# Bonus sums behind the preparation, a new column order of the key tile, and small copies on GpSimd, in a hybrid RWKV-7 and RG-LRU block

## The chip, the core and the metric

The kernel runs on one core of a Trainium2 chip. The metric is device microseconds of one execution, lower is better. Five engines take part, each with its own queue of instructions: TensorE (PE, matrix products; PEld is its loading of weights), VectorE (DVE), ScalarE (ACT), GpSimd (POOL) and SyncE (SP, which only issues transfers here). DMA transfers move data between the chip's memory (HBM) and the core's on-chip memory (SBUF); products land in PSUM, of which the kernel uses eight banks of 128 partitions by 512 floats. Instructions on an engine run in their queue's order; semaphores order the engines among each other.

## What is computed

The block maps x (512 frames by 1024 channels, float32) through a mixer with two branches, a cross-attention to 256 memory rows and a gated convolutional feed-forward layer. The change lies in the first branch, RWKV-7, with 8 heads of 64 channels:

```python
p = p + (token_shift(p) - p) * mu
r, k, v = p[..., :c0], p[..., c0:c1], p[..., c1:c2]
...
w_log = -jax.nn.softplus(-(w0 + jnp.tanh(pw) @ w_up)) - 0.5
decay = jnp.exp(-jnp.exp(w_log))
a = jax.nn.sigmoid(a0 + pa @ a_up)
...
kk = k * k_k
k = k * (1.0 + (a - 1.0) * k_a)
...
kk = kk / jnp.maximum(jnp.sqrt(jnp.sum(kk * kk, axis=-1, keepdims=True)), 1e-12)
y = rwkv7_recurrence(r, decay, k, v, -kk, kk * a)
...
y = ((y - mean) * lax.rsqrt(var + LNX_EPS)).reshape(bsz, s, A_WIDTH) * lnx_g + lnx_b
bonus = jnp.sum(r * k * r_k, axis=-1, keepdims=True) * v
return (y + bonus.reshape(bsz, s, A_WIDTH)) * g
```

The recurrence is S_t = S_{t-1} diag(w_t) + (S_{t-1} a_t) b_t^T + v_t k_t^T with y_t = S_t r_t, where −kk stands for a and kk·a for b. The keys k and the "betas" b = kk·a of the title are the last two factors of the recurrence; the bonus is a sum over a head's 64 channels, times v. The second branch is a causal convolution with a gated linear recurrence (RG-LRU). Both are merged by gates, and the rest of the block follows.

## The kernel before

**Layout.** Activations lie channels by frames. Four pairs of heads (j = 0 to 3) fill 128 partitions each, one head (e = 0 or 1) in each half. The 512 frames are cut into 8 chunks of 64.

**Projections.** `inproj(i)` computes 128 output columns of `h @ w_in` into one PSUM tile `in_ps{i}`: 24 matmuls, since each float32 product is made of three with rounded parts (high times high, high times low, low times high; lines 160 to 162). A weight tile arrives by DMA (`win_r`), is rounded on ACT (`win_h`, L114), and DVE subtracts for the low part (`win_l`, L115); three buffers hold the high parts and three the low ones. Tiles `in_ps` share three PSUM banks. `evac_shift` (L521 to L525) evacuates one: it fills column 0 of `q` (L523), ACT writes the shifted rest of `q` (L524), and DVE combines `q` with the PSUM tile (L525) into `pk` (k), `pr` (r) or `vT` (v). `q` has two buffers, which `sq` uses too. The columns are taken in the order 12, 13, 4, 5, 0, 1, 8, 9 (k, r, v of pairs 0 and 1), 6, 7, 2, 3, 10, 11 (pairs 2 and 3), then the other branches' from 22 on.

**Preparation of a pair.** `prep(j)` makes the low-rank products `psw` and `psa` (L547, L548, four matmuls), the cumulated log decay by a scan (L553), its exponentials `Pp` and `L` and the decay of each chunk, `PC` (L558). `prep2(j)` normalises kk (the sum `ss`, L156 and L157), and fills `AK` (the left factors: −kk and r with decay) and `KBt` (betas and keys with the inverse decay), each split by chunk. `scores(j)` multiplies `KBt` by `AK`, chunk by chunk, into four PSUM tiles `sc{j}_{e}_{cg}`, and DVE masks each twice (L609 into `BZ`, L610 into `AK`). `bonus(j)` multiplies r, k and `r_k` (L586), sums over each head on PE in two parts (`sum_exact`: high part on ACT, low on DVE, two matmuls, L154 to L157), multiplies by v (L589), adds `lnx_b` and stores to `dBo[j]` in HBM. The low-rank products, sums and scores share four PSUM banks (tag `rw`).

**Then.** After the four pairs, DVE inverts 32 by 32 triangles (Z, the `zh` and `zo` products combine them), while PE goes on with projections. The chunk loop runs the recurrence: `rows_v` and `rows_kb` transpose a chunk's v and `KBt` on PE (the latter at L746), `chunk` makes `x` from the state and `AK`, then `u`, the state's update `s` (L781) and the output `y`; `Sn` (L791) and the sums into the next `UV` (L795) carry the state on. `group_norm` reads `dBo` later.

**The order.** A scheduler puts each engine's instructions into one static order when the kernel is built, by its own estimates; regions in `tc.high_priority` go first. Between the projections POOL issues sums over weights of the feed-forward layer, as accumulating DMA transfers into `dS` (L425), so many for each projection as `NSUM` says. Such a sum also waits for the earlier transfer into the same tile.

Of the kernel before, what the change touches and what calls it, by code (L numbers as in the profile page):

```python
# [17 lines left out]
P = 128  # L18
# [35 lines left out]
def hybrid_block_kernel(ctx: ExitStack, tc: tile.TileContext, xT_d, mT_d, pv_d, cst_d, win_d, wk_d, wv_d,  # L54
# [423 lines left out]
    pa_ctx = ExitStack()  # L478
    pa = pa_ctx.enter_context(tc.tile_pool(name="pa", bufs=1, reuse_waits="tile"))
    BZ = pa.tile([P, NPAIR * NC, P], F32, tag="AR", name="BZ")  # L480
    KBt = big.tile([P, NPAIR, 2 * NC + 1, HD], F32, tag="x16", name="KBt")
    vT = pa.tile([P, NPAIR, T], F32, name="vT")
    AK = pa.tile([P, 2, NPAIR * NC, P], F32, tag="SC", name="AK")
    PC = pa.tile([P, NPAIR, NC], F32, name="PC")
# [35 lines left out]

    def evac_shift(ps, blk, out):  # L521
        q = pp.tile([P, T], F32, tag="q", name=f"q{blk}", bufs=2)
        V.tensor_copy(q[:, 0:1], qb[:, blk:blk + 1])  # L523
        S.activation(q[:, 1:T], ps[:, 0:T - 1], AF.Identity, scale=par("mu", blk), bias=par("b_in", blk))  # L524
        V.scalar_tensor_tensor(out, ps, omu[:, blk:blk + 1], q, ALU.mult, ALU.add)  # L525

# [16 lines left out]
    def prep(j):  # L543
        sl = slice(j * P, (j + 1) * P)
        psw, psa = rw_ps(f"psw{j}"), rw_ps(f"psa{j}")
        for i, ps in enumerate((psw, psa)):
            PE.matmul(ps, lhi[:, i, sl], pwa[i], start=True, stop=False)  # L547
            PE.matmul(ps, llo[i][:, sl], pwa[i], start=False, stop=True)  # L548
        L = pp.tile([P, T], F32, tag="L", name=f"L{j}")
        tab(L, psw, AF.Sigmoid, bias=par("w0", j))  # L550
        at = pp.tile([P, T], F32, tag="at", name=f"at{j}")
        tab(at, psa, AF.Sigmoid, bias=par("a0", j))
        V.tensor_tensor_scan(L, smask, L, 0.0, ALU.mult, ALU.add)  # L553
# [4 lines left out]
        V.tensor_copy(PC[:, j, :], Pp[:, :, HD])  # L558
        return at, L, Pp

    def prep2(j, pk, pr, at, Pi, Pp):
        c3 = lambda a: a.rearrange("p (c t) -> p c t", t=HD)
        kk = pp.tile([P, T], F32, tag="kk", name=f"kk{j}")
        S.activation(kk, pk, AF.Copy, scale=par("k_k", j))
        sq = pp.tile([P, T], F32, tag="q", name=f"sq{j}", bufs=2)
        S.activation(sq, kk, AF.Square)
        ps = rw_ps(f"ss{j}")
        sum_exact(ps, bonesr, sq, tp, "xb", f"ss{j}")
        tab.rsqrt(sq, ps, 1.0, eps[:, 2:3])
        V.scalar_tensor_tensor(kk, sq, 1e12, kk, ALU.min, ALU.mult)  # L570
# [4 lines left out]
        V.tensor_tensor(kk, kk, at, ALU.mult)  # L575
        V.tensor_tensor(KBt[:, j, 1::2, :], c3(kk), c3(Pi), ALU.mult)
        S.activation(at, at, AF.Identity, scale=par("k_a", j), bias=oka[:, j:j + 1])
        V.tensor_tensor(pk, pk, at, ALU.mult)
        V.tensor_tensor(KBt[0:HD, j, 2::2, :], c3(pk)[0:HD], c3(Pi)[0:HD], ALU.mult)
        V.tensor_tensor(KBt[HD:P, j, 0:2 * NC:2, :], c3(pk)[HD:P], c3(Pi)[HD:P], ALU.mult)  # L580
        for e in range(2):
            hs = half[e]
            V.tensor_tensor(AK[hs, e, jc, HD:P], c3(pr)[hs], Pp[hs, :, 1:], ALU.mult)

    def bonus(j, pk, pr):
        V.scalar_tensor_tensor(pr, pr, par("r_k", j), pk, ALU.mult, ALU.mult)  # L586
        ps = rw_ps(f"bo{j}")
        sum_exact(ps, bonesr, pr, tp, "xb", f"bo{j}")
        V.tensor_tensor(pr, ps, vT[:, j, :], ALU.mult)  # L589
        S.activation(pr, pr, AF.Identity, bias=par("lnx_b", j))  # L590
        nc.scalar.dma_start(dBo[j], pr)

    def kb_cols(j, e, c):
        return KBt[half[e], j, 2 * c + 1 - e:2 * c + 3 - e, :].rearrange("p a t -> p (a t)")

    def scores(j):
        for e in range(2):
            hs, oh = half[e], half[1 - e]  # L600
            for cg in range(2):
                ps = rw_ps(f"sc{j}_{e}_{cg}")
                i0 = j * NC + cg * 4
                for i in range(4):
                    PE.matmul(ps[:, i * P:(i + 1) * P], kb_cols(j, e, cg * 4 + i), AK[hs, e, i0 + i, :],
                              start=True, stop=True)
# [3 lines left out]
                V.tensor_tensor(AK[oh, e, i0:i0 + 4, :], p3[oh], m3[oh], ALU.mult)  # L610
# [10 lines left out]
    for jp in range(2):  # L621
        js = (2 * jp, 2 * jp + 1)
        pks, prs = {}, {}
        for j in js:
            pks[j] = pp.tile([P, T], F32, tag="pk", name=f"pk{j}", bufs=2)
            evac_shift(inproj(4 + j), 4 + j, pks[j])
        for j in js:
            prs[j] = pp.tile([P, T], F32, tag="pr", name=f"pr{j}", bufs=3)
            evac_shift(inproj(j), j, prs[j])
        for j in js:  # L630
            evac_shift(inproj(8 + j), 8 + j, vT[:, j, :])
        for j in js:
# [12 lines left out]


    with tc.tile_pool(name="pz", bufs=1, reuse_waits="tile") as pz:
# [91 lines left out]
        return UV  # L739

    def rows_kb(c):
        KBr = ch.tile([P, 2, NPAIR, HD], F32, tag="KBr", name=f"KBr{c}", bufs=2)
        for e in range(2):
            ps = ch_ps(f"kbr{c}_{e}", ("kv", "s")[e])
            for j in range(NPAIR):
                PE.transpose(ps[:, j * HD:(j + 1) * HD], kb_cols(j, e, c), ident[half[e], half[e]])  # L746
            S.copy(KBr[:, e], j3(ps[:, 0:256]))
        return KBr

    def pc_b(c):  # L750
# [2 lines left out]
    def chunk(c, UV, KBr, SP):  # L753
# [22 lines left out]
        if not last:  # L776
            nUV = rows_v(c + 1)
            pss = ch_ps(f"s{c}", "s")
            for j in range(NPAIR):
                for e in range(2):  # L780
                    PE.matmul(pss[half[e], j * HD:(j + 1) * HD], KBr[:, e, j, :], UV[:, e, j, :],  # L781
                              start=True, stop=True)
        for j in range(NPAIR):
            for e in range(2):
# [633 lines left out]
```

## Time and profile before

| | |
|---|---|
| time, median of 3 runs (lowest to highest) | 911.82 us (911.26 to 913.13) |
| the profiled execution, its span in the profile | 909.73 us, 908.0 us |
| mean granted clock of TensorE | 0.998 |
| preparation of the pairs | about 100 to 200 us of the span |
| bonus (L156, L157 on `bo`) | 8 matmuls, first at 119.30 us |
| transposes of `KBt` (L746) | 64 matmuls, 7.8 us busy |

An execution takes a little longer than its span, which goes from the first to the last recorded instruction. Busy time counts an engine's instructions; a matmul's end is modelled, so matmuls overlap in the record, and what one costs is read from start to start. In a timeline row stand the start, the duration, the engine, the line, the operation, the output and inputs, and in brackets the idle time of the engine ahead of it with what ended it.

### The profile page before, as it was taken

Reading aid. Unit: us, or ns where it says so; the run is one execution under the profiler, and the core shown is the slowest. Engines: PE = TensorE matmul, PEld = TensorE weight load, DVE = VectorE, ACT = ScalarE, POOL = GpSimd, SP = SyncE. Lnnn points to the kernel's source line nnn. Section 1 sums busy time; section 2 is a strip of 40 time slices with the busy share of each in tenths; the row PEclk is TensorE's granted clock in tenths of the full one; section 3 lists DMA queues with packets and bytes.
Section 4 is the critical chain, followed back from the end, with each engine's and each line's share of the span. In section 5 each row is a group of like instructions: output and inputs, shape, how many; then the busy total and the mean of one; then the engine's idle time right before and its main releaser. Section 6 shows DMA issues by size and latency. Waiting matters only on the chain. (4 is left out here: it accounts for less than half of the span.)

```text
span 908.0 us, 15914 instructions
## 1 busy us (share of the span) xinstructions
PE 890.5 (98%) x6218; PEld 776.1 (85%) x6218; DVE 687.4 (76%) x1096; ACT 510.4 (56%) x779; POOL 129.3 (14%) x159
## 2 busy tenths in 40 slices
PE   7999999999999999999999999999999999999996
PEld 6988877788877777887887778999999999999996
DVE  7884598776957585776565568788998888999674
ACT  6674675542236675234454446765665556767663
POOL 0102222010011212001112211111111111201100
PEclk9999999999999999999999999999999999999999
DMA  8878899667499749858788868898989998998963
GB/s 276 277 263 230 186 237 208 179 165 206 139 205 246 167 106 194 258 180 223 210 243 190 177 152 185 240 273 247 280 249 290 258 316 251 248 277 222 269 197 93
DMA packets 102411, 200.07 MB, mean 220 GB/s; under 512 B 25344, under 2 KB 36736, under 8 KB 102272
## 3 DMA queue, kind: packets, MB, share of 16 engines
q1 hardware_dynamic: 69504, 119.75, 41.0%
q0 software_dynamic: 25504, 67.38, 36.8%
q10 hardware_dynamic: 7328, 11.92, 3.9%
q8 instruction: 49, 0.80, 0.3%
q14 instruction: 26, 0.21, 0.1%
HBM read 187.75 MB, written 77.59 MB: 292 GB/s over the span
## 5 line engine op out<-in xcount | busy, mean ns | idle before, releaser
L126 ACT CAST wfi_h<-wfi_r 128x1024 fp32r<-128x1024 f32 x77 | 81.0, 1052 | 76.8 <-PE fx_ps L161 21.1
L160 PE MATMUL in_ps<-hT,win_h 128*128 128x512 f32 x304 | 121.9, 402 | 0.8 <-DVE pr L525 0.7
L162 PE MATMUL in_ps<-hT,win_l 128*128 128x512 f32 x304 | 120.8, 398 | 0.0
L161 PE MATMUL in_ps<-hT,win_h 128*128 128x512 f32 x304 | 120.6, 398 | 0.0
L127 DVE TENSOR_TENSOR wfi_l<-wfi_r,wfi_h 128x1024 fp32r<-128x1024 f32 x77 | 94.0, 1221 | 23.5 <-ACT wfi_h L126 23.3
L425 POOL DMA_DIRECT2D dS<-in_wfi x66 | 66.5, 1044 | 267.0 <-PE in_ps L160 132.4
L114 ACT CAST win_h<-win_r 128x1024 fp32r<-128x1024 f32 x38 | 39.8, 1048 | 71.9 <-PE in_ps L161 70.9
L115 DVE TENSOR_TENSOR win_l<-win_r,win_h 128x1024 fp32r<-128x1024 f32 x38 | 46.4, 1221 | 32.6 <-ACT win_h L114 32.5
L160 PEld LDWEIGHTS in_ps<-hT,win_h 128*128 128x128 f32 x304 | 57.0, 187 | 15.6 <-DVE pr L525 1.1
L161 PEld LDWEIGHTS in_ps<-hT,win_h 128*128 128x128 f32 x304 | 57.0, 188 | 14.0 <-issue 0.7
L162 PEld LDWEIGHTS in_ps<-hT,win_l 128*128 128x128 f32 x304 | 57.0, 187 | 13.9 <-issue 0.2
L461 POOL DMA_DIRECT2D dOs<-in_wfo x54 | 39.9, 804 | 186.0 <-PE fx_ps L160 50.9
L1245 DVE TENSOR_TENSOR wfo_l<-wfo_r,wfo_h 128x1024 fp32r<-128x1024 f32 (+1 forms) x39 | 47.2, 1210 | 13.6 <-ACT wfo_h L1244 13.5
L1244 ACT CAST wfo_h<-wfo_r 128x1024 fp32r<-128x1024 f32 (+1 forms) x39 | 40.4, 1038 | 28.2 <-PE oyz_ps L161 9.8
L161 PE MATMUL fx_ps<-hr,wfi_h 128*128 128x256 f32 x176 | 49.7, 282 | 0.0
L162 PE MATMUL fx_ps<-hr,wfi_l 128*128 128x256 f32 x176 | 49.7, 282 | 0.0
L160 PE MATMUL ox_ps<-go,wfo_h 128*128 128x256 f32 x176 | 49.6, 282 | 0.1
L160 PE MATMUL fyz_ps<-hq,wfi_h 128*128 128x256 f32 x176 | 49.3, 280 | 0.4 <-ACT p L1173 0.4
L160 PE MATMUL fx_ps<-hq,wfi_h 128*128 128x256 f32 x176 | 49.5, 281 | 0.0
L160 PE MATMUL fx_ps<-hr,wfi_h 128*128 128x256 f32 x176 | 49.4, 281 | 0.0
L162 PE MATMUL ox_ps<-go,wfo_l 128*128 128x256 f32 x176 | 49.3, 280 | 0.0
L161 PE MATMUL ox_ps<-go,wfo_h 128*128 128x256 f32 x176 | 49.3, 280 | 0.0
(418 smaller groups left out, 2727.8 us busy)
## 6 DMA issues: line engine op xcount, KB each, us to landing
dS<-in_wfi POOLq DMA_DIRECT2D x66, 512.0 KB, 8.4
wfi_r<-dS SPq DMA_DIRECT2D x44, 512.0 KB, 6.9
win_r<-in_win SPq DMA_DIRECT2D x38, 512.0 KB, 5.0
wfi_r<-in_wfi SPq DMA_DIRECT2D x33, 512.0 KB, 5.6
dS<-dS POOLq DMA_DIRECT2D x22, 512.0 KB, 5.7
dOs<-in_wfo POOLq DMA_DIRECT2D x12, 512.0 KB, 7.8
wv_r<-in_wv SPq DMA_DIRECT2D x8, 512.0 KB, 4.9
dG<-gs ACTq DMA_DIRECT2D x16, 256.0 KB, 2.6
```

The costliest lines, as they stand in the source:

```text
L114: S.copy(hi[:, o:o + n], raw[:, o:o + n])
L115: V.tensor_tensor(lo[:, o:o + n], raw[:, o:o + n], hi[:, o:o + n].bitcast(F32), ALU.subtract)
L126: S.copy(hi, raw)
L127: V.tensor_tensor(lo, raw, hi.bitcast(F32), ALU.subtract)
L160: first = PE.matmul(ps, lh, rh, start=start, stop=False, **kw)
L161: PE.matmul(ps, lh, rl, start=False, stop=False, **kw)
L162: PE.matmul(ps, ll, rh, start=False, stop=stop, **kw)
L425: return lambda: nc.gpsimd.dma_start(s(out), src, **kw)
L461: yield lambda k=k, w=w, src=src: nc.gpsimd.dma_start(dO[n, m][:, k * P:(k + w) * P], src, **kw)
L1244: S.copy(hi[:, :n], raw[:, :n])
L1245: V.tensor_tensor(lo[:, :n], raw[:, :n], hi[:, :n].bitcast(F32), ALU.subtract)
```

## The change

It has three parts.

1. *KBt.* Each chunk now has two blocks of 64 columns without the overhang of one block. In the low half of the partitions (head e = 0) the beta stands first and the key second, in the high half the other way. So both blocks of a chunk, all 128 partitions, can be transposed at once: `rows_kb` makes one whole 128 by 128 transpose a pair into one PSUM tile (tag `kv`) and one copy of 512 columns, where it made two of 64 partitions into two tiles (tags `kv` and `s`) and two copies of 256 columns. `KBt` is written by four operations on half the partitions for each pair, where it was one on all and two on halves.
2. *Bonus.* In the preparation `bonus_terms` forms the product and stores it to `dBo`; `bonus`, for all pairs behind the preparation, loads it back, sums, multiplies by v, adds and stores. The loaded tile takes the tag `ga`, two buffers.
3. *Copies.* The copy of `q`'s first column (14 times), the fill of `Pp`'s first column and the copy of `PC` (4 times each) go from DVE to GpSimd.

```diff
-    KBt = big.tile([P, NPAIR, 2 * NC + 1, HD], F32, tag="x16", name="KBt")
+    KBt = big.tile([P, NPAIR, 2 * NC, HD], F32, tag="x16", name="KBt")
...
-        V.tensor_copy(q[:, 0:1], qb[:, blk:blk + 1])
+        nc.gpsimd.tensor_copy(q[:, 0:1], qb[:, blk:blk + 1])
...
-        V.memset(Pp[:, :, 0:1], 1.0)
+        nc.gpsimd.memset(Pp[:, :, 0:1], 1.0)
...
-        V.tensor_copy(PC[:, j, :], Pp[:, :, HD])
+        nc.gpsimd.tensor_copy(PC[:, j, :], Pp[:, :, HD])
...
-        V.tensor_tensor(KBt[:, j, 1::2, :], c3(kk), c3(Pi), ALU.mult)
         S.activation(at, at, AF.Identity, scale=par("k_a", j), bias=oka[:, j:j + 1])
         V.tensor_tensor(pk, pk, at, ALU.mult)
-        V.tensor_tensor(KBt[0:HD, j, 2::2, :], c3(pk)[0:HD], c3(Pi)[0:HD], ALU.mult)
-        V.tensor_tensor(KBt[HD:P, j, 0:2 * NC:2, :], c3(pk)[HD:P], c3(Pi)[HD:P], ALU.mult)
+        for e in range(2):
+            hs = half[e]
+            V.tensor_tensor(KBt[hs, j, e::2, :], c3(kk)[hs], c3(Pi)[hs], ALU.mult)
+            V.tensor_tensor(KBt[hs, j, 1 - e::2, :], c3(pk)[hs], c3(Pi)[hs], ALU.mult)
...
-    def bonus(j, pk, pr):
+    def bonus_terms(j, pk, pr):
+
         V.scalar_tensor_tensor(pr, pr, par("r_k", j), pk, ALU.mult, ALU.mult)
+        nc.scalar.dma_start(dBo[j], pr)
+
+    def bonus(j):
+        bt = tp.tile([P, T], F32, tag="ga", name=f"bt{j}", bufs=2)
+        nc.scalar.dma_start(bt, dBo[j])
         ps = rw_ps(f"bo{j}")
-        sum_exact(ps, bonesr, pr, tp, "xb", f"bo{j}")
-        V.tensor_tensor(pr, ps, vT[:, j, :], ALU.mult)
-        S.activation(pr, pr, AF.Identity, bias=par("lnx_b", j))
-        nc.scalar.dma_start(dBo[j], pr)
+        sum_exact(ps, bonesr, bt, tp, "xb", f"bo{j}")
+        V.tensor_tensor(bt, ps, vT[:, j, :], ALU.mult)
+        S.activation(bt, bt, AF.Identity, bias=par("lnx_b", j))
+        nc.scalar.dma_start(dBo[j], bt)
...
-    def kb_cols(j, e, c):
-        return KBt[half[e], j, 2 * c + 1 - e:2 * c + 3 - e, :].rearrange("p a t -> p (a t)")
+    def kb_cols(j, hs, c):
+        return KBt[hs, j, 2 * c:2 * c + 2, :].rearrange("p a t -> p (a t)")
...
-            bonus(j, pks[j], prs[j])
+            bonus_terms(j, pks[j], prs[j])
...
+    for j in range(NPAIR):
+        bonus(j)
...
-        KBr = ch.tile([P, 2, NPAIR, HD], F32, tag="KBr", name=f"KBr{c}", bufs=2)
-        for e in range(2):
-            ps = ch_ps(f"kbr{c}_{e}", ("kv", "s")[e])
-            for j in range(NPAIR):
-                PE.transpose(ps[:, j * HD:(j + 1) * HD], kb_cols(j, e, c), ident[half[e], half[e]])
-            S.copy(KBr[:, e], j3(ps[:, 0:256]))
+        KBr = ch.tile([P, NPAIR, P], F32, tag="KBr", name=f"KBr{c}", bufs=2)
+        ps = ch_ps(f"kbr{c}", "kv")
+        for j in range(NPAIR):
+            PE.transpose(ps[:, j * P:(j + 1) * P], kb_cols(j, slice(0, P), c), ident)
+        S.copy(KBr, ps.rearrange("p (j i) -> p j i", i=P))
```

In `scores` and in the state's update `s` only the indices follow the new layout.

The scheduler places more than the lines that were edited. On TensorE, around the scores of pair 1 (`sc1`; `bo1` is that pair's bonus sum, `in_ps10` the projection block for v of pair 2), this stands before, the blocks of 24 cut to their rows at the edges:

```order
L160 MATMUL in_ps10_1392<-hT2_0_89,win_h12_1395 128x512
L161 MATMUL in_ps10_1392<-hT2_1_90,win_h12_1395 128x512
L605 MATMUL sc1_0_0_1199<-AK_746,KBt_744 128x128 x4
L605 MATMUL sc1_1_1_1221<-AK_746,KBt_744 128x128 x4
L156 MATMUL bo1_1230<-bo1_h_1231,bonesr_80 128x512
L162 MATMUL in_ps10_1392<-hT2_0_89,win_l12_1396 128x512
L162 MATMUL in_ps10_1392<-hT2_0_89,win_l12_1396 128x512
L547 MATMUL psw2_1466<-pwa0_807,lhi_763 128x512
L548 MATMUL psa2_1467<-pwa1_808,llo1_765 128x512
L157 MATMUL bo1_1230<-bo1_l_1232,bonesr_80 128x512
```

And after the change, where `sc1` follows the last matmul of `in_ps3`:

```order
L162 MATMUL in_ps3_1339<-hT2_0_89,win_l11_1343 128x512
L613 MATMUL sc1_0_0_1192<-AK_746,KBt_744 128x128 x4
L613 MATMUL sc1_1_1_1214<-AK_746,KBt_744 128x128 x4
L547 MATMUL psw2_1450<-pwa0_807,lhi_763 128x512
L548 MATMUL psa2_1451<-pwa1_808,llo1_765 128x512
L160 MATMUL in_ps10_1376<-hT2_0_89,win_h12_1379 128x512
```

The scores have moved from the middle of `in_ps10` to ahead of it, the low-rank products of pair 2 too, and the bonus sum has gone to behind the preparation.

On VectorE, around the `KBt` operations of pair 1 (`pr2` is the evacuation of `in_ps2`, `pk3` that of `in_ps7`), before:

```order
L525 SCALAR_TENSOR_TENSOR pr2_1316<-in_ps2_1317,dp_672,q2_1350 128x512
L115 TENSOR_TENSOR win_l14_1553<-win_r14_1550,win_h14_1552 128x1024
L576 TENSOR_TENSOR KBt_744<-kk1_1175,L1_1163 128x8x64
L579 TENSOR_TENSOR KBt_744<-pk1_892,L1_1163 64x8x64
L580 TENSOR_TENSOR KBt_744<-pk1_892,L1_1163 64x8x64
L586 SCALAR_TENSOR_TENSOR pr1_966<-pr1_966,pv_75,pk1_892 128x512
L609 TENSOR_TENSOR BZ_743<-sc1_0_0_1199,cst_76 64x512
L610 TENSOR_TENSOR AK_746<-sc1_1_1_1221,cst_76 64x512
L525 SCALAR_TENSOR_TENSOR pk3_1278<-in_ps7_1279,dp_672,q7_1312 128x512
```

And after:

```order
L580 TENSOR_TENSOR KBt_744<-kk1_1167,L1_1155 64x8x64 x2
L577 TENSOR_TENSOR pk1_892<-pk1_892,at1_1158 128x512
L115 TENSOR_TENSOR win_l14_1529<-win_r14_1526,win_h14_1528 128x1024
L581 TENSOR_TENSOR KBt_744<-pk1_892,L1_1155 64x8x64 x2
L588 SCALAR_TENSOR_TENSOR pr1_966<-pr1_966,pv_75,pk1_892 128x512
L617 TENSOR_TENSOR BZ_743<-sc1_0_0_1192,cst_76 64x512
L618 TENSOR_TENSOR AK_746<-sc1_1_1_1214,cst_76 64x512
L525 SCALAR_TENSOR_TENSOR pk3_1262<-in_ps7_1263,dp_672,q7_1296 128x512
L525 SCALAR_TENSOR_TENSOR pr2_1300<-in_ps2_1301,dp_672,q2_1334 128x512
```

The evacuations of `in_ps7` and `in_ps2` now stand next to each other behind the last mask of `sc1` (L618, before L610); before, that of `in_ps2` stood ahead of the `KBt` operations. A weight's low part (`win_l14`, the first block of column 22) stands between the betas and the keys.

On GpSimd's queue, which held only the sums here, after the change (`q7`, `q2`, `q3` are the tiles of the evacuations of `in_ps7`, `in_ps2`, `in_ps3`):

```order
L558 COPY PC_747<-Pp1_1161 128x8
L425 DMA dS1_718<-in_wfi 128x2x512
L425 DMA dS0_717<-in_wfi 128x2x512
L523 COPY q7_1296<-dp_672 128x1
L425 DMA dS1_718<-in_wfi 128x2x512
L425 DMA dS1_718<-dS1_718 128x2x512
L523 COPY q2_1334<-dp_672 128x1
L425 DMA dS2_719<-in_wfi 128x2x512
L425 DMA dS1_718<-in_wfi 128x2x512
L425 DMA dS1_718<-dS1_718 128x2x512
L523 COPY q3_1372<-dp_672 128x1
```

Each copy waits in this queue for the sums ahead of it.

More of the change, by code (lines that the diff above doesn't have):

```diff
@@ L604, in scores @@
                 for i in range(4):
-                    PE.matmul(ps[:, i * P:(i + 1) * P], kb_cols(j, e, cg * 4 + i), AK[hs, e, i0 + i, :],
+                    PE.matmul(ps[:, i * P:(i + 1) * P], kb_cols(j, hs, cg * 4 + i), AK[hs, e, i0 + i, :],
                               start=True, stop=True)
@@ L780, in chunk @@
                 for e in range(2):
-                    PE.matmul(pss[half[e], j * HD:(j + 1) * HD], KBr[:, e, j, :], UV[:, e, j, :],
+                    PE.matmul(pss[half[e], j * HD:(j + 1) * HD], KBr[:, j, half[e]], UV[:, e, j, :],
                               start=True, stop=True)
```

## The prediction, made blind

> **What bounds the kernel now.** I read the page's busy times first, then the busy times by stage, and last the timelines of TensorE, VectorE and ScalarE over the stretch where the change rewrites the order. The columns of the stage rows are the stretch, its length, the busy us and instruction counts of PE, PEld, DVE, ACT and POOL, the granted clock, the DMA share and the GB/s.
>
> ```profile
> PE 890.5 (98%) x6218; PEld 776.1 (85%) x6218; DVE 687.4 (76%) x1096; ACT 510.4 (56%) x779; POOL 129.3 (14%) x159
> 100.00:125.00 25.00, 24.45 (x122) 19.68 (x121) 20.63 (x30) 17.12 (x22) 5.72 (x6) 1.00 0.89 203
> 125.00:150.00 25.00, 23.72 (x116) 18.32 (x115) 23.93 (x43) 16.75 (x23) 5.49 (x7) 1.00 0.95 212
> 150.00:175.00 25.00, 24.77 (x123) 19.86 (x122) 19.82 (x29) 14.61 (x21) 3.02 (x3) 1.00 0.80 213
> ...
> 300.00:325.00 25.00, 25.00 (x417) 18.50 (x416) 16.16 (x36) 19.29 (x39) 3.73 (x4) 1.00 0.64 121
> ```
>
> TensorE is the bound: 890.5 of 908.0 us, in the chunk loop (300 to 325) without a gap, at a full clock. Between 100 and 150, where the first two head pairs are prepared, it misses 0.55 + 1.28 us, and DVE is almost as full: 23.93 of 25 us in the second stretch. So two things decide: how much PE work the change removes, and whether in the new static order DVE, which is nearly full here, still serves PE in time.
>
> **Prep: the waits that the new order opens.** The rows give start, duration, engine, line, operation and tiles; brackets show an idle time before and who ended it.
>
> ```profile
> 115.25 3.50 PE L605 MATMUL sc<-AK,KBt 64*128 64x128 f32 x32
> 119.30 0.47 PE L156 MATMUL bo<-bo_h,bonesr 128*128 128x512 f32 x1 [0.55 <-DVE AK L610]
> ...
> 133.74 0.50 PE L160 MATMUL in_ps<-hT,win_h 128*128 128x512 f32 x1 [0.67 <-DVE pr L525]
> 134.08 0.39 PE L161 MATMUL in_ps<-hT,win_h 128*128 128x512 f32 x1
> 134.31 0.39 PE L162 MATMUL in_ps<-hT,win_l 128*128 128x512 f32 x1
> ...
> 137.25 3.47 PE L605 MATMUL sc<-AK,KBt 64*128 64x128 f32 x32
> ...
> 145.41 0.50 PE L160 MATMUL in_ps<-hT,win_h 128*128 128x512 f32 x1 [0.17 <-DVE pk L525]
> ```
>
> Projection matmuls start 0.23 us apart (134.08, 134.31), so a block of 24 (one in_ps tile) is 5.6 us. In before, TensorE has fourteen matmuls of block 10 ahead of sc1, the scores of pair 1, and ten behind it: work that covers DVE. The order in the section on the change shows that cover gone: sc1 stands directly behind block 3, and block 10 behind sc1 and four low-rank matmuls. Block 10 used to take the PSUM bank of block 2 (evacuated into pr at 132.94); now it takes the bank of block 7, whose evacuation (pk3) stands on DVE behind all eight masks of sc1. I walk the new order with durations of before:
>
> ```profile
> 113.19 0.68 DVE L576 TENSOR_TENSOR KBt<-kk,L 128x512 f32<-128x512 f32 x1
> ...
> 114.51 0.69 DVE L579 TENSOR_TENSOR KBt<-pk,L 64x512 f32<-64x512 f32 x1
> ...
> 115.95 0.75 DVE L586 SCALAR_TENSOR_TENSOR pr<-pr,pv,pk 128x512 f32<-128x512 f32 x1
> ...
> 117.22 1.21 DVE L115 TENSOR_TENSOR win_l<-win_r,win_h 128x1024 fp32r<-128x1024 f32 x1
> 118.45 0.70 DVE L610 TENSOR_TENSOR AK<-sc,cst 64x512 f32<-64x512 f32 x1
> ...
> 123.26 0.67 DVE L155 TENSOR_TENSOR bo_l<-pr,bo_h 128x512 fp32r<-128x512 f32 x1
> 123.86 1.21 DVE L553 TENSOR_TENSOR_SCAN L<-cst,L 128x512 f32<-128x512 f32 x1
> 125.00 0.12 DVE L523 COPY q<-dp 128x1 f32<-128x1 f32 x1
> 125.04 0.67 DVE L589 TENSOR_TENSOR pr<-bo,vT 128x512 f32<-128x512 f32 x1
> 125.64 0.73 DVE L525 SCALAR_TENSOR_TENSOR pk<-in_ps,dp,q 128x512 f32<-128x512 f32 x1
> 126.30 0.15 DVE L558 COPY PC<-Pp 128x8 f32<-128x8 f32 x1
> ...
> 126.97 1.38 DVE L583 TENSOR_TENSOR AK<-pr,Pp 64x512 f32<-64x512 f32 x2
> ...
> 132.34 0.68 DVE L575 TENSOR_TENSOR kk<-kk,at 128x512 f32<-128x512 f32 x1
> 132.88 1.04 ACT L114 CAST win_h<-win_r 128x1024 fp32r<-128x1024 f32 x1 [0.69 <-PE in_ps L161]
> ```
>
> - sc0 starts as before, 115.3: its first half needs the two KBt operations of the low half only, ready at about 115.2. It ends at 118.8.
> - DVE then has the other two KBt operations (the new layout takes four half-partition operations of 0.69 a pair, where three stood), pr 0.75 and the weight's low part 1.21, and starts the masks at 118.45, as before. Seven masks lie between 118.45 and 123.26, 0.69 each; eight end at 123.95, the scan at 125.1, the low part of ss1 at 125.7, pk2 at 126.4.
> - PE: 54 matmuls stand between sc0 and sc1 (blocks 2 and 3, four low-rank ones, two sums): 12.6 us. They wait for PSUM of masked scores as bo0 did at 119.30 (0.55), here 0.45 before the first low-rank one and 0.6 before the first sum. Block 3 ends at 118.8 + 12.6 + 1.05 plus half a us of restarts, as those that 133.74 to 134.08 shows, **132.9**.
> - DVE, which also waits for PE and ACT in this time, gets through the two AK groups (1.38 each), kk, kk·at, two KBt operations and k·at by 134.6. Ahead of the KBt of k stands the low part of a later weight, and its cast on ACT frees only with the last matmul that used the buffer, now that of block 3 (in before the cast at 132.88 waits for TensorE in the same way): 132.9 + 0.5 + 1.04 is 134.45, the low part 1.21 more to 135.85 with its overlap, KBt 0.69: 136.5. **sc1 waits 3.6 us.**
> - sc1 takes 3.5, to 140.05, and the low-rank ones end at 141.4. DVE's eight masks start after pr at 138.0 and end at 143.65, pk3 0.73 behind them: block 10 starts at 144.5. **A second wait of 3.1 us.**
> - Compare at one place: in before block 11 starts at 145.41, with block 10 (5.6) and four bonus matmuls (0.95) done. In after that is 144.5 + 5.6 + 0.95, or 151.05: **+5.6 us**. It is less than 3.6 + 3.1, since before's own waits of 0.55, 0.67 and 0.17 go there.
>
> For pairs 2 and 3 the same walk finds no new wait: more blocks stand between the scores there. In the stretch from 150 to 175 DVE has 19.82 us of work in 25 and catches up.
>
> What leaves DVE per pair is bo_l 0.67 and the bonus product 0.67 (to the later bonus), copies of 0.12 to 0.15 and a fill; one KBt operation comes. That relief is in the walk already. It doesn't help where DVE waits for a cast.
>
> **GpSimd's queue.**
>
> ```profile
> L425 POOL DMA_DIRECT2D dS<-in_wfi x39 | 38.9, 1048 | 167.9 <-PE in_ps L160 132.4 <-issue 12.9 <-DMA dS<-dS 8.4
> L1407 POOL MEMSET const-float32-0.0<- 128x1 f32 x1 | 0.1, 98 | 0.2 <-issue 0.2
> ...
> dS<-in_wfi POOLq DMA_DIRECT2D x66, 512.0 KB, 8.4
> dS<-dS POOLq DMA_DIRECT2D x22, 512.0 KB, 5.7
> ```
>
> POOL has no copy that reads SBUF in this trace; the nearest row is a one-column fill of 0.10 us, so 22 operations are 2.2 us on an engine that is 14% busy. Queued among them are the paced sums of the weight (each 1.05 us to issue), and a sum waits for an earlier transfer to land, medians of 8.4 and 5.7 us from issue to landing (the last column of the two lower rows). The copies q2 and q3 stand behind two and three such landings; q3 would be done between 147 and 153, and the evacuation that needs it is reached at 146. DVE has other work to about 150. From 0 to 4 us; I take **+0.3**, near the lower end, for the cover.
>
> On ports: the Trainium skill, "SBUF — State Buffer", section "SBUF: two separate sides", says that a GpSimd operation and a DVE operation with two SBUF inputs exclude each other for the whole instruction when the GpSimd one reads SBUF. No run here shows it yet; at 18 copies of the fill's 0.10 us DVE would lose up to 1.8 us (an estimate, with nothing of it in the sum).
>
> **The bonus, later.** Its four sums stand behind the preparation, with a store and a load between product and sum, and two buffers for four pairs. The work for PE is the same eight matmuls. bo1_l waits behind one low part of a weight (1.21), and the third and fourth load wait for a buffer. Waits of 0 to 2 us, **+0.8**, two thirds of a low part. Nothing is costed for the following Z stage.
>
> **Chunk loop.**
>
> ```profile
> L746 PE MATMUL kbr<-cst,KBt 64*128 64x64 f32 x64 | 7.8, 237 | 0.0
> 293.66 0.46 PE L746 MATMUL kbr<-cst,KBt 64*128 64x64 f32 x4
> 294.05 0.50 PE L160 MATMUL in_ps<-hT,win_h 128*128 128x512 f32 x1
> ...
> 484.00 0.82 PE L1028 MATMUL prT_ps<-cst,ex 128*128 128x128 f32 x4
> 484.58 0.36 PE L1016 MATMUL sc_ps<-K,q 128*128 128x256 f32 x1
> ...
> 315.03 0.42 DVE L791 TENSOR_TENSOR Sn<-s,PC 128x256 f32<-128x256 f32 x1 [1.49 <-PE s L781]
> 315.49 0.87 DVE L795 TENSOR_TENSOR UV<-Sn,SP 64x256 f32<-64x256 f32 x2
> ...
> 316.35 0.33 PE L759 MATMUL x<-UV,AK 128*64 128x64 f32 x3
> ```
>
> Sixteen groups of four 64-row transposes go, each 0.39 us from start to start (293.66 to 294.05), 6.25 us. In come 32 whole ones in eight groups of four. The nearest row is that of the whole transposes of the attention, four in 0.58 (484.00 to 484.58). I take 0.39, as for the 64-row ones: a group moves as many columns through TensorE, and the attention's group also changes over from other shapes. Eight are 3.1: **−3.2**, with ends −1.6 (0.58 a group) and −4.7 (half of 0.39). By the two orders TensorE changes between projections and small matmuls 106 times in place of 114 in the stages up to the chunk loop's end; a change costs 0.11 (133.74 to 134.08 is 0.34, the next step 0.23), so **−0.9**, or nothing if groups in a row hide it.
>
> Where the transposes go, a wait can come. Sn and its two sums on DVE run from 315.03 to 316.36, and x, which reads them, starts at 316.35: no slack, and one group of transposes (0.39) is part of what TensorE does in between. In the new order it isn't there in most chunks. Seven chunks give 0 to 2.7; projections stand there in some, so I take **+1.0**.
>
> On transposes the Trainium skill, "TensorE: Matmul & The Clock Gate", Part 4, states about 275 ns for a 128 by 128 bf16 transpose inside a kernel. 32 of these would be 8.8 us, more than the 6.25 removed, and the sum +9.3 instead of +3.6. The row above disagrees from start to start: four in 0.58 are 0.145 each.
>
> **Sum.** +5.6 + 0.3 + 0.8 − 3.2 − 0.9 + 1.0 = **+3.6 us**. The profiled execution took 909.73 us (span 908.0), so 913.3; the median of the three runs shown is 911.82, 2.1 above it, and with the same difference the forecast is **915.4**.
>
> **Rivals.**
> - *The walk is too strict.* The casts or masks end earlier than worked out and half of the two waits stay: −2.8, 912.6 (911 to 914). For it: DVE's rows overlap by up to 0.1 each. Against: the cast can't start before block 3 has ended. 0.17. That the relief of DVE isn't what it says (four KBt operations for three) is in the walk.
> - *GpSimd becomes the wait.* q2 or q3 stands behind a sum whose transfer lands late: the evacuation and its PSUM bank come 2 to 4 later, 918.4 (917 to 920). For it: the landings of 5.7 to 8.4. Against: POOL had slack in before. 0.11.
> - *Faster: the relief of DVE closes both waits.* If DVE reaches sc1's KBt 3.6 us earlier than worked out, which needs the cast to find its buffer free before block 3 ends, sc1 follows block 3 at once, the masks and pk3 end in time, and the waits of before (0.55, 0.67, 0.17) go too: −1.4 for +5.6, a sum of −3.4: 908.4 (905 to 910). Pair 0, where the KBt operations meet block 7 in time, behaves like that. 0.12.
> - *Whole transposes that nothing overlaps.* At the full 0.82 of the group at 484.00, eight take 6.6 and gain nothing: +3.3, 918.7. Against: in that very row the next matmul starts after 0.58. 0.03.
>
> **How the numbers follow.** Forecast 0.57 (914 to 917, by the nearer ends of the small terms), the rivals 0.17, 0.11, 0.12 and 0.03. A measurement of this kernel tells about 0.2% from no change, 1.8 us: faster is below 910.0, slower above 913.6. Faster 0.12; most of the first rival makes 0.15 the same; slower is the rest, 0.73. The range leaves out the faster rival and the upper end of GpSimd's, some 0.17: 910 to 919.
>
> **What would show it.** In the profile after: brackets of 3 to 4 us before the scores of pair 1 (released by DVE's KBt) and before block 10 (released by pk3); block 11 starting near 151; eight groups of whole transposes of 0.2 to 0.6 each; waits of x for the sum on UV. Wrong it is if TensorE runs through 130 to 150 without a gap, if pk3's q copy on POOL is the one waited for, or if groups of whole transposes take over 0.8.

## The result, and the profile after

| | before | after |
|---|---|---|
| time, median of 4 runs (lowest to highest) | 912.15 us (911.26 to 913.13) | 925.58 us (924.87 to 926.84) |
| profiled execution, span | 909.73, 908.0 us | 926.84, 925.1 us |
| mean granted clock | 0.998 | 0.989 |

The change made the kernel slower by 13.4 us, a ratio of 1.0153 with a 95% interval of 1.0136 to 1.017. The forecast was slower by 3.6, in a range that ended at 919.

The page's busy times of the changed kernel, then its longest waits of TensorE (us in total, times, longest), then the busy times by stage in the columns of the prediction:

```profile
PE 895.5 (97%) x6186; PEld 779.7 (84%) x6186; DVE 688.8 (74%) x1078; ACT 509.9 (55%) x771; POOL 136.5 (15%) x181
PE bo L156 <- ACT bo_h L154: 6.7, 1, 6.7
PE k_ps L160 <- ACT m L286: 6.4, 2, 6.2
PE sc L613 <- DVE KBt L581: 3.3, 1, 3.3
PE ss L156 <- ACT ss_h L154: 2.1, 1, 2.1
PE in_ps L160 <- DVE pk L525: 0.7, 1, 0.7
125.00:150.00 25.00, 20.86 (x86) 16.39 (x85) 21.03 (x29) 13.59 (x18) 7.56 (x10) 0.80 0.82 176
...
200.00:250.00 50.00, 43.27 (x190) 34.57 (x189) 33.61 (x71) 15.75 (x21) 2.32 (x2) 0.93 0.66 179
```

The busy time of DVE and ACT hardly moves. Three waits are new: at the scores of pair 1 (sc), at a sum of pair 2 (ss), and 6.7 us at a late bonus sum (bo). The one at k_ps, ahead of all this, is in both kernels (6.2 before). The stretch from 125 to 150 has a granted clock of 0.80 where before it had 1.00, and that from 200 to 250 has 0.93.

To see where the time goes, I read in each trace's timeline when TensorE starts the first of the 24 matmuls of a projection block, and subtract what the kernel before has. In the order of blocks, 12 is the first, 11 lies behind the scores of pair 1, 25 behind those of pair 2, 31 behind the late bonus; yb is the first product behind the chunk loop. In us, with the runs of the next section; the last three columns are measured times, their distance from the kernel before as it was measured beside them, and the ratio:

| kernel | 12 | 11 | 25 | 31 | yb | time | over before | ratio to before, interval |
|---|---|---|---|---|---|---|---|---|
| after | +1.7 | +7.4 | +9.2 | +19.7 | +16.6 | 925.58 | +13.4 | 1.0153 (1.0136 to 1.0170) |
| copies back on DVE | −0.1 | −1.3 | −2.3 | +8.9 | +5.8 | 915.76 | +5.0 | 1.0064 (1.0047 to 1.0081) |
| PC alone back on DVE | −0.4 | −1.9 | −1.0 | +9.6 | +6.2 | 918.60 | +7.9 | 1.0093 (1.0067 to 1.0119) |
| small copies on ACT | +0.1 | −1.2 | −2.1 | +6.9 | +4.2 | 915.50 | +4.8 | 1.0045 (1.0020 to 1.0070) |
| bonus early | +0.1 | +6.1 | +14.6 | +15.1 | +12.6 | 924.22 | +13.4 | 1.0161 (1.0138 to 1.0184) |
| layout alone | +0.4 | +4.5 | +4.4 | +4.5 | +2.0 | 911.44 | +0.6 | 1.0014 (0.9998 to 1.0030) |
| layout, copies on ACT | −1.0 | +7.3 | +7.8 | +8.6 | +6.2 | 918.46 | +7.7 | 1.0087 (1.0065 to 1.0109) |
| copies alone | +0.8 | +1.8 | +11.9 | +14.2 | +13.7 | 927.49 | +16.7 | 1.0195 (1.0163 to 1.0227) |
| copies without PC | −0.1 | +6.4 | +6.6 | +8.8 | +7.8 | 921.67 | +11.2 | 1.0126 (1.0097 to 1.0156) |
| copies, sums later | +0.2 | −2.4 | −2.9 | −0.6 | +13.5 | 928.13 | +17.7 | 1.0202 (1.0183 to 1.0221) |
| before, sums later | +1.6 | +1.6 | +1.6 | +1.6 | +12.9 | 921.66 | +11.2 | 1.0116 (1.0099 to 1.0133) |
| late bonus in YB | −0.4 | −1.5 | −2.5 | −1.2 | +2.5 | 914.85 | +4.4 | 1.0045 (1.0026 to 1.0064) |
| all three, on ACT and in YB | +0.1 | −1.2 | −2.1 | −0.7 | +2.5 | 916.05 | +5.3 | 1.0068 (1.0042 to 1.0093) |

The kernel before took 912.15 beside the changed one and 910.45 to 910.80 beside the later runs, so kernels are compared by their distance from it. The time of the last row leaves out one slow run of 928.57. Column 12 lies ahead of everything that the change touches on TensorE: its spread of −1.0 to +1.7 differs from execution to execution (the kernel with only sums moved has +1.6), and the 1.7 of after belongs to that execution. Without it, after loses 5.7 up to block 11, 1.8 more to block 25, 10.5 more to block 31, and gains 3.0 to yb.

**The first loss, pair 1.** TensorE's timeline, then the windows there:

```profile
137.53 4.96 PE L613 MATMUL sc<-AK,KBt 64*128 64x128 f32 x32 [3.29 <-DVE KBt L581]
142.43 0.79 PE L547 MATMUL psw<-pwa,lhi 128*128 128x512 f32 x1
...
145.17 0.77 PE L160 MATMUL in_ps<-hT,win_h 128*128 128x512 f32 x1 [0.67 <-DVE pk L525]
...
146.16 0.63 PE L162 MATMUL in_ps<-hT,win_l 128*128 128x512 f32 x1
146.59 0.63 PE L160 MATMUL in_ps<-hT,win_h 128*128 128x512 f32 x1
...
137.00:140.00 3.00, 2.47 (x22) 2.50 (x23) 2.92 (x5) 0.00 (x0) 0.61 (x2) 0.87 0.96 225
140.00:143.00 3.00, 3.00 (x13) 2.70 (x13) 2.89 (x6) 0.00 (x0) 0.00 (x0) 0.50 1.07 304
143.00:146.00 3.00, 2.33 (x6) 1.42 (x5) 2.97 (x5) 2.07 (x3) 0.00 (x0) 0.50 1.04 378
...
149.00:152.00 3.00, 3.00 (x13) 2.39 (x13) 0.00 (x0) 0.00 (x0) 0.00 (x0) 0.92 1.06 141
```

sc1 waits 3.29 for DVE's KBt, and then takes 4.96 where it took 3.47: from 140 to 149 the granted clock is 0.50. The steps of block 10 are 0.43 apart up to 149.15, not 0.23.

**The second, pair 2.** GpSimd's timeline, with the evacuation on DVE that waits for it:

```profile
127.38 0.19 POOL L558 COPY PC<-Pp 128x8 f32<-128x8 f32 x1 [12.89 <-ACT Pp L237]
127.62 2.33 POOL L425 DMA_DIRECT2D dS<-in_wfi  x2
129.04 1.75 POOL L523 COPY q<-dp 128x1 f32<-128x1 f32 x1
129.17 2.71 POOL L425 DMA_DIRECT2D dS<-in_wfi  x1
135.67 0.72 POOL L425 DMA_DIRECT2D dS<-dS  x1 [3.79 <-DMA dS<-in_wfi]
...
147.03 1.17 POOL L425 DMA_DIRECT2D dS<-in_wfi  x1 [9.42 <-DMA dS<-dS]
154.39 0.71 POOL L425 DMA_DIRECT2D dS<-dS  x1 [6.18 <-DMA dS<-in_wfi]
155.09 0.20 POOL L523 COPY q<-dp 128x1 f32<-128x1 f32 x1
155.32 0.75 DVE L525 SCALAR_TENSOR_TENSOR pr<-in_ps,dp,q 128x512 f32<-128x512 f32 x1 [8.51 <-POOL q L523]
```

The copy of PC stands first in GpSimd's queue and waits 12.89 us for the exponentials on ACT. Three sums that had been due go out behind it in a bunch (127.62 to 131.9). The sums that follow wait for landings: 3.79, 9.42 and 6.18 us. The q copy of block 3 (155.09) is behind the third, and DVE idles 8.51 us for it. In the kernel before, GpSimd's queue held nothing here but the sums themselves, so these landings held up no copy.

**The third, the late bonus.** ACT's timeline, with the issues of its DMA queue (ACTq):

```profile
207.16 0.33 ACTq L598 DMA_DIRECT2D dBo<-bt  x1
...
215.25 0.33 ACTq L593 DMA_DIRECT2D bt<-dBo  x1
215.62 0.69 ACT L237 ACTIVATE gs<-in_ps,pv 128x512 f32<-128x512 f32 x1 [4.01 <-DMA dBo<-bt]
...
217.41 0.55 ACTq L593 DMA_DIRECT2D bt<-dBo  x1
222.43 0.62 ACT L154 CAST bo_h<-bt 128x512 fp32r<-128x512 f32 x1 [6.12 <-DMA bt<-dBo]
```

The third product is loaded (215.25) into the buffer that the store of 207.16 reads, so it waits until that store has landed; ACT's queue stands still for 4.01 us ahead of the gate's sigmoid at 215.62. The cast at 222.43 then waits 6.12 for the load's landing. TensorE waits 6.73 for it at 223.10, and works at half speed again.

### The profile page after: what moved, and what is told of

It reads as the page before. It is cut to its first block, busy times and chain, and to the rows that moved or that the text cites. A ratio compares the mean times of both kernels' runs of the same rounds, so it can differ in the third digit from the quotient of the medians.

```text
span 925.1 us, 15898 instructions
## 1 busy us (share of the span) xinstructions
PE 895.5 (97%) x6186; PEld 779.7 (84%) x6186; DVE 688.8 (74%) x1078; ACT 509.9 (55%) x771; POOL 136.5 (15%) x181
## 4 chain that ended last, share of the span: by engine, by line
PE 85%; DMA 8%; DVE 4%; ACT 1%; issue 1%; SPq 0%; DVEq 0%; POOL 0%; ACTq 0%; POOLq 0%
PE in_ps L160 7%; PE in_ps L161 7%; PE in_ps L162 6%; PE fx_ps L161 5%; PE fx_ps L160 5%; PE fx_ps L162 5%; PE fyz_ps L161 3%; PE fyz_ps L162 3%; PE fyz_ps L160 3%; DMA wfo_r<-dOs 2%; PE mix_ps L160 2%; PE co_ps L162 2%; PE q_ps L161 2%; PE mix_ps L161 2%; PE mix_ps L162 2%; PE co_ps L161 2%
## 5 line engine op out<-in xcount | busy, mean ns | idle before, releaser
L160 PE MATMUL in_ps<-hT,win_h 128*128 128x512 f32 x304 | 123.3, 407 | 0.7 <-DVE pk L525 0.7
L161 PE MATMUL in_ps<-hT,win_h 128*128 128x512 f32 x304 | 122.0, 403 | 0.0
L160 PEld LDWEIGHTS in_ps<-hT,win_h 128*128 128x128 f32 x304 | 58.1, 191 | 15.4 <-ACT L L237 1.4
L161 PEld LDWEIGHTS in_ps<-hT,win_h 128*128 128x128 f32 x304 | 58.1, 191 | 14.3 <-issue 0.7
L1255 DVE TENSOR_TENSOR wfo_l<-wfo_r,wfo_h 128x1024 fp32r<-128x1024 f32 (+1 forms) x39 | 47.1, 1208 | 14.6 <-ACT wfo_h L1254 14.4
```

Source lines behind the costliest of these rows:

```text
L160: first = PE.matmul(ps, lh, rh, start=start, stop=False, **kw)
L161: PE.matmul(ps, lh, rl, start=False, stop=False, **kw)
L1255: V.tensor_tensor(lo[:, :n], raw[:, :n], hi[:, :n].bitcast(F32), ALU.subtract)
```

## The experiments

Two theories stood at the start. The one: three separate costs, each the price of a new wait (the place of sc1 in the order, the bonus's round trip, GpSimd's queue), against a gain of 3 us from the transposes. The rival: one part, the late bonus or the layout's extra KBt operation, makes nearly all of it.

### Copies back on DVE

```diff
-        nc.gpsimd.tensor_copy(q[:, 0:1], qb[:, blk:blk + 1])
+        V.tensor_copy(q[:, 0:1], qb[:, blk:blk + 1])
...
-        nc.gpsimd.memset(Pp[:, :, 0:1], 1.0)
+        V.memset(Pp[:, :, 0:1], 1.0)
...
-        nc.gpsimd.tensor_copy(PC[:, j, :], Pp[:, :, HD])
+        V.tensor_copy(PC[:, j, :], Pp[:, :, HD])
```

> The change with the small copies and fills back on DVE; new key layout and late bonus stay. Theory (three separate costs: the place of the scores of pair 1 about +7.5 with its slow clock, the bonus round trip about +9.5, transposes -3): the order has eight matmuls of block 10 ahead of sc1 again, so the wait there shrinks below 1.5 us and its clock stays full, the bonus wait of 6 to 7 us stays: 917 to 921. Rival (the fourth KBt operation of the layout makes the wait of sc1, wherever the copies run): the wait of 3 us and the low clock stay, 924 to 926.

915.76 us, 5.0 over before where the whole change is 13.4 over it: 8.5 us hang on 22 operations of a few elements. The waits at sc1 and ss are gone, and the one at the bonus is the longest of TensorE:

```profile
PE bo L156 <- ACT bo_h L154: 7.7, 1, 7.7
```

The order has eight matmuls of block 10 ahead of sc1 again. The fourth KBt operation is still there, so by itself it isn't what makes sc1 wait.

### Bonus early

The bonus is again as in the kernel before; layout and GpSimd copies stay.

> The change with the bonus as before, in the preparation; new key layout and GpSimd copies stay. Theory: sc1 still stands directly behind block 3 in the order and waits about 3 us, with a slow clock behind it, and the evacuation of block 3 waits for its copy on GpSimd; no wait in the bonus: before +7 +2 -3, 915 to 919. Rival (the late bonus is the whole loss): 908 to 910.

924.22 us, above the theory's range, and the rival falls. Without the late bonus the time is the same, 13.4 over before, because GpSimd's copies cost more here (+14.6 at block 25, where the whole change has +9.2). Its longest waits of TensorE in the preparation and DVE's waits for GpSimd are

```profile
PE ss L156 <- ACT ss_h L154: 5.6, 1, 5.6
PE sc L606 <- DVE KBt L581: 4.2, 1, 4.2
...
DVE pr L525 <- POOL q L523: 6.9, 2, 5.7
DVE vT L525 <- POOL q L523: 4.3, 1, 4.3
```

### Layout alone

> The new key layout and the whole transposes alone; bonus and copies as before. Theory: thirteen matmuls of block 10 cover sc1, no new wait in the preparation, the chunk loop 3 us shorter: 908 to 910. Rival (whole transposes cost as much as the pairs of halves, or x waits for what they covered): 911.5 to 913.

911.44 us, the same as before. The chunk loop gains (from block 31 to yb −2.4), but the preparation loses 4: the order differs there too, and block 3 waits for pk (PE's timeline, then the window behind it, at half speed):

```profile
129.58 0.50 PE L160 MATMUL in_ps<-hT,win_h 128*128 128x512 f32 x1 [1.82 <-DVE pk L525]
130.00:133.00 3.00, 3.00 (x9) 2.30 (x8) 2.78 (x5) 2.91 (x4) 0.72 (x1) 0.54 0.84 199
```

So the theory was right on the chunk loop and wrong on the preparation.

### Copies alone

The kernel before with the small copies and fills on GpSimd, nothing else.

> The copies and fills on GpSimd alone; old layout, bonus as before. Theory (a copy on GpSimd stands behind sums that wait for a transfer to land): a copy of the second pairs' evacuation comes late by some us, DVE idles for it and TensorE loses 1 to 4 us, 913 to 916. Rival (the copies are free, what they take from DVE is gained): 910.5 to 912.5.

927.49 us, 16.7 above before and no less than the whole change. The theory named the mechanism and had its size far too low. GpSimd's timeline, with DVE's evacuation and TensorE's sum behind it:

```profile
153.04 0.72 POOL L425 DMA_DIRECT2D dS<-dS  x1 [5.11 <-DMA dS<-in_wfi]
162.40 1.83 POOL L425 DMA_DIRECT2D dS<-in_wfi  x2 [8.64 <-DMA dS<-dS]
163.97 0.97 POOL L425 DMA_DIRECT2D dS<-dS  x1
164.67 0.46 POOL L523 COPY q<-dp 128x1 f32<-128x1 f32 x1
165.16 0.75 DVE L525 SCALAR_TENSOR_TENSOR vT<-in_ps,dp,q 128x512 f32<-128x512 f32 x1 [9.63 <-POOL q L523]
169.31 0.80 PE L156 MATMUL ss<-ss_h,bonesr 128*128 128x512 f32 x1 [8.95 <-ACT ss_h L154]
```

The sum at 162.40 waits 8.64 us for a landing, the q copy is behind it, DVE idles 9.63, and TensorE 8.95 for what DVE and ACT make next.

### Is it the queue or the copies?

Two runs take the queue apart: one puts the copy of PC back on DVE, one takes the sums out of the stretch. The second needs a control, since moved sums meet other transfers.

```diff
-    NSUM = {12: 1, 13: 1, 4: 1, 5: 1, 0: 1, 1: 1, 8: 1, 9: 1, 6: 2, 7: 2, 2: 2, 3: 2, 10: 2, 11: 2,
-            22: 2, 23: 1, 27: 1, 28: 1, 29: 1, 15: 4, 16: 4, 17: 4, 18: 4, 19: 4, 20: 3, 21: 2}
+    NSUM = {12: 1, 13: 1, 4: 1, 5: 1, 0: 1, 1: 1, 8: 1, 9: 1, 22: 2, 23: 1, 27: 1, 28: 1, 29: 1, 30: 2, 31: 2, 32: 1, 33: 1, 34: 1, 35: 1, 36: 1, 37: 1, 14: 2, 15: 4, 16: 4, 17: 4, 18: 4, 19: 4, 20: 3, 21: 2}
```

> Copies only (old layout, bonus as before), but the copy of PC back on DVE: q's column copies and the fills stay on GpSimd. Theory (the PC copy waits 13 us for the exponentials on ACT and holds up the sums behind it, which then come in a bunch, each waiting for the last one's landing, with the q copies behind them): without it the sums go out as before and the q copies come in time, 910 to 915. Rival (any copy behind a sum that waits for a landing is late, PC or not): DVE still idles 5 us or more for a q copy, 919 to 927.

921.67 us, 11.2 over before: 5.5 less than with PC, so its wait counts, but the rival holds as well. DVE waits 4.94 for a q copy on GpSimd here, and sc1 5.0 for DVE.

> Copies only, all on GpSimd, but no weight sums are issued beside projection blocks 6, 7, 2, 3, 10 and 11; those twelve go to the blocks of columns 30 to 37 and 14. Theory (the copies are late only because of the sums ahead of them in GpSimd's queue): each copy runs when its input is there, no wait for a copy on DVE, within 2 us of the kernel before with its sums moved in the same way, 909 to 914. Rival (the copies themselves, or the order that the scheduler makes of them, cost the time): 920 or more.

> The kernel before with the twelve sums moved in the same way, nothing else: the control for the run above. Theory: the sums are transfers that nothing waits for before the feed-forward layer, 909 to 913. Rival (moved sums collide with the transfers of the Z stage): 914 or more.

928.13 and 921.66 us: the control shows that the moved sums themselves cost 11, so the times don't decide. The stages do. In both, TensorE waits long at zh, for the transfer that brings the Z stage's inverse (copies with sums later, then the control):

```profile
PE zh L687 <- DMA ZA<-dZt: 6.4, 1, 6.4
```

```profile
PE zh L686 <- DMA ZA<-dZt: 7.0, 1, 7.0
```

Ahead of it, up to block 31, the copies with no sums beside them stand at −0.6 (from +14.2 with the sums), and no instruction waits for one of the fourteen q copies. In this answer on the tile q, the durations are 183, 186 and 714 ns at the least, the median and the most, and the list of who waited for it is empty:

```profile
L522 POOL COPY q<-dp x14: 183/186/714, 5.9 to 147.4; 128x1 f32<-128x1 f32 x14
...
who waited for it (us, times):
```

So the copies are cheap, and the queue makes them late. What the whole time of that kernel loses beyond its control lies behind block 31; its trace has waits of 3.0 (at ga, L853) and 3.3 (at the attention's scores, L1016) there that the control's hasn't, and no run separates them.

### The whole change with PC back on DVE

> The whole change with only the copy of PC back on DVE; q's column copies and the fills stay on GpSimd. The order has sc1 inside block 10 again. Theory (a copy behind a sum that waits for a landing is late, and DVE with it): sc1's scheduled cover returns, but DVE still idles 4 us or more for a q copy and TensorE waits at sc1 or at the sum of pair 2; bonus wait as in the change: 919 to 924. Rival (PC's wait of 13 us alone spoils GpSimd's queue): as with all copies back, 914 to 917.

918.60 us, between the two ranges and 7.9 over before: one of the three kinds of copy carries 5.6 of the 8.5 us. In the order sc1 has thirteen matmuls of block 10 ahead of it again, since the scheduler placed it so once PC left GpSimd; the lag at block 25 falls from +9.2 to −1.0, and DVE waits 1.9 for a q copy. So PC's copy both held up the sums and moved sc1. These two are not separated by this run.

### The whole change with the copies on ACT

The same copies as `S.copy`, the fill on DVE.

> The whole change with the copies of q's column and of PC on ACT in place of GpSimd, the fill back on DVE. DVE is relieved as in the change, but nothing stands behind the sums. Theory (GpSimd's queue makes the loss in the preparation): no wait over 2.2 us there, the bonus wait of 6 to 8 us stays: 914 to 917. Rival (taking the copies off DVE changes the order so that sc1 and block 10 come too early): waits of 3 us in the preparation remain, 920 or more.

915.50 us, as with the copies on DVE, and the preparation is at −2.1: relieving DVE does no harm by itself. What is left up to block 31 is the bonus (a wait of 5.5).

### Late bonus without the shared buffers

`bt` is a tile of tag `ga` for pairs 0 and 1 and `YB[:, j, :]` for 2 and 3.

```diff
-        bt = tp.tile([P, T], F32, tag="ga", name=f"bt{j}", bufs=2)
+        bt = (tp.tile([P, T], F32, tag="ga", name=f"bt{j}", bufs=2) if j < 2 else YB[:, j, :])
```

> New layout and late bonus, copies on DVE (the run with copies back), but the loaded products of pairs 2 and 3 lie in the then unused tile YB, so that their loads don't wait for the stores of pairs 0 and 1. Theory (the bonus wait of 7.7 us is the chain store of pair 0 lands, load of pair 2 into its buffer, landing, cast): the wait falls under 3 us and the time to 906 to 910, faster than before. Rival (the round trip of the last product itself, store then load on ACT's queue, sets it): the wait moves to the sum of pair 1 or 3 and keeps 5 us or more, 912 to 916.

The wait of 7.7 us is gone altogether and the lag at block 31 falls from +8.9 to −1.2: the buffer was the cause. But the time is 914.85, 4.4 over before, within the noise of the 5.0 with the wait: in the rival's range, though not by its mechanism. TensorE's two longest waits are now

```profile
PE k_ps L160 <- ACT m L286: 6.3, 1, 6.3
PE zh L697 <- DMA ZA<-dZt: 4.3, 1, 4.3
```

It comes to zh earlier, and the Z stage's chain (the load of the masked scores, DVE's inversion, its store and load) isn't there yet. That chain had little slack in the kernel before. The first zh rows of TensorE, before and with YB:

```profile
266.45 1.19 PE L687 MATMUL zh<-ZA,BZ 32*32 32x32 f32 x32
```

```profile
267.01 1.31 PE L697 MATMUL zh<-ZA,BZ 32*32 32x32 f32 x32 [4.31 <-DMA ZA<-dZt]
```

Before, the first of the two loads of the inverse lands at 265.57 us, and zh starts 0.9 behind it without a wait. With YB it lands at 266.97, although the last mask of the scores ended no later (193.39, before 194.16): what comes earlier on TensorE waits here. Of the 10 us at block 31, 3 are left at yb in the profiled executions, and fewer in the medians.

### The version that the runs pointed to

Layout and late bonus with YB, copies on ACT; and, to see whether a relieved DVE keeps the layout's gain, the layout with copies on ACT and the early bonus.

> The whole change with the small copies on ACT and the loaded products of pairs 2 and 3 in YB, so that neither GpSimd's queue nor the stores stand in the way. Theory (late bonus, layout and relief each gain when their waits are gone): 906 to 911. Rival (the Z stage's chain through DVE and its transfers then is the bound and TensorE waits at zh for 3 us or more, as in the run with YB): 912 to 916.

> The new layout with the small copies on ACT, bonus as before in the preparation. Theory (with DVE relieved, the layout's gain of 2 to 3 us in the chunk loop is kept, and the 4 us that the layout alone lost in the preparation goes): 906 to 910. Rival (the preparation is bound by the order around pairs 0 and 1, not by small copies on DVE): 911 to 914.

916.05 and 918.46 us, the first at the end of its rival's range, the second above its rival's. The first waits 3.4 at zh. In the second, order again: block 10 waits 5.46 for an evacuation (pr) that stands on DVE behind the kk operations, and then runs at half speed:

```profile
137.02 0.79 PE L160 MATMUL in_ps<-hT,win_h 128*128 128x512 f32 x1 [5.46 <-DVE pr L525]
```

No version here beats the kernel before; the layout alone equals it.

## Why the prediction was wrong, point by point

Without the opening's 1.7, the sum and the trace compare like this by stage: up to block 11, +4.7 forecast and +5.7 measured; to block 25, +0.3 and +1.8; to block 31, +1.8 (0.8, and the 0.95 of moved matmuls) and +10.5; to yb, −3.1 and −3.0. (That is 15.0 in the profiled execution, the slowest of four; the medians differ by 13.4.) So the step that failed most is the late bonus, taken for a wait of 0 to 2 us; the walk's full clock and GpSimd's queue follow.

- **sc1's place: right, and its wait.** 3.6 us were forecast, 3.29 came, released by KBt as said. The part that reads the order and walks it with durations of before holds up to that wait.
- **The walk's durations: a failed assumption.** It ran on with sc1 at 3.5 us and blocks of 5.6 us "with durations of before", which are those of a full clock. After the wait sc1 took 4.96 and the next nine matmuls of block 10 some 0.43 each. That is 1.5 + 2.0, and some 0.8 on the four low-rank products: about 4 us that no term held. In turn the second wait was 0.67, not 3.1: TensorE was slower to get there. So it was in part luck that block 11 started 5.7 late after the opening's 1.7 (the forecast, by +5.6 less the 0.95 of bonus work still to come, was 4.7).
- **GpSimd, +0.3: mis-sized, and one half of its mechanism was not seen.** The row of 14% busy time and "cover to about 150" were taken for slack. The q copy came at 155.1, at 153.4 without the opening's 1.7, just past the late end that was forecast, and that cost 2.3 us of waits at ss (2.11 and 0.23). What was not seen is PC: its copy waits 12.89 us at the head of the queue and all sums behind it wait too. By undoing, the copies cost 8.5 us of the 13.4 and PC 5.6 of these, but this holds the lost cover of sc1, which the walk had as its own term; alone on the old kernel they cost 16.7. The second rival had this mechanism, at a chance of 0.11 and a price of 3 more.
- **The bonus, +0.8, "waits of 0 to 2": the term that failed most.** The wait was 6.73, and the loss up to block 31 was 10.5 with the slow clock and the 0.95 of moved matmuls. The text says that loads wait for a buffer, but priced it by a weight's low part on DVE (1.21) where the row to take was a transfer's landing, of several us: from the store at 207.16 to the cast at 222.43 it is 15.3. In the whole time undoing it is worth less: nothing with the copies on GpSimd (13.4 over before with it and without it, since the copies then cost more), and 4.3 without them (911.44 to 915.76).
- **The chunk loop, −3.2 −0.9 +1.0: right in sum.** From block 31 to yb it is −3.0 in after, −2.4 in the layout alone. The terms were not right one by one. Of the eight groups of four whole transposes three stay together; they take 0.59 from start to start once, as in the attention's row (0.58), and 0.41 twice, near the 0.39 that was taken:

```profile
306.30 0.66 PE L756 MATMUL kbr<-cst,KBt 128*128 128x128 f32 x4
306.89 0.62 PE L769 MATMUL x<-UV,AK 128*64 128x64 f32 x13
...
310.37 0.66 PE L756 MATMUL kbr<-cst,KBt 128*128 128x128 f32 x4
310.78 0.48 PE L160 MATMUL in_ps<-hT,win_h 128*128 128x512 f32 x1
...
L756 PE MATMUL kbr<-cst,KBt 128*128 128x128 f32 x32 | 6.4, 296 | 0.0
L769 PE MATMUL x<-UV,AK 128*64 128x64 f32 x128 | 7.7, 231 | 0.2
```

  The order splits the other five in two parts each. All 32 take 4.4 from start to start, where the 64 of before take 6.5 (two of their sixteen groups are split too): a saving of 2.1, not 3.2. The waits of x are 0.2 in all, not 1.0. The rest of the 3.0, some 1.1, would be the fewer changes between projections and small products (0.9 forecast), which no run measured alone.
- **The rivals.** The faster one needed the cast to find its buffer before block 3 had ended; it didn't. "Whole transposes that nothing overlaps" fell by the rows above: 0.59 at most, not 0.82. Its +3.3 should read +3.5 by its own terms, as the walk's 135.85 should read 135.66 (134.45 + 1.21); neither slip decides anything.

The slow clock belongs to a rule that was at hand. The Trainium skill, "TensorE: Matmul & The Clock Gate", Part 1 on the clock gate, says that TensorE's clock falls to one half after an idle window of about 3.4 us and comes back after one that is busy. The traces agree in kind: granted 0.50 behind the waits of 3.29 and 6.73. They differ in the threshold: 1.82 was enough in the layout-alone run, while 1.89 later in that run and 2.11 in after were not. Worked out with the rule, the walk would have been dearer from the first wait on.

## What to carry to other kernels

A small operation that is moved to an idle engine takes that engine's queue with it: before costing it, list what stands ahead of it there, what each of these waits for (here a transfer's landing of 4 to 9 us), and what it itself will hold up while it waits. When a walk through a new order finds a wait of TensorE of 3 us or more, cost the matmuls behind it at half speed as well. When a load goes into a buffer that a store still reads, price it by the landing of that store and then its own. And a wait that is taken away in one stage is a gain only if the next stage's chain isn't as long: here 10 us at the bonus became 3 or fewer behind the Z stage. For the same reason costs found by undoing one part at a time don't add up to the whole.

## What the runs showed of the hardware

- After every wait of TensorE of 3.0 us or more behind the first 60 us (3.0 to 9.0 in these runs) the granted clock was 0.50 for some 3 to 13 us, and projection matmuls ran 0.43 apart in it, not 0.23. Of four waits of about 2 us, two had this behind them (1.82 in the layout alone, 2.13 in the copies alone) and two had not (1.89 in the layout alone, 2.11 in after). The longest such times, 10 to 13 us, followed waits at or just ahead of the scores of pair 1; why they last longer is not shown. No run here held the clock up through a wait, so its share is read from the steps, not from an experiment.
- A copy of one column took 0.18 to 0.71 us on GpSimd in the run with the sums moved, and up to 1.75 beside the issue of two sums (129.04 in after), where the fills of `Pp` took 0.11 to 0.13 in the preparation of pairs 1 and 2. DVE's operations did not get longer (KBt 0.68 to 0.69 before, 0.67 to 0.69 in after, one of them beside a copy at 136.38).
- Twelve sums of 512 KB, issued beside blocks 30 to 37 and 14 in place of the six blocks of pairs 2 and 3, cost 11 us, with the load of the inverse late (zh waited 7.0): transfers that nothing waits for are not free where they run.
